# Moving half of the gated attention's values between two groups of output gates, and pacing its side work by columns

## The chip, the cores and the metric

The kernel runs on one core of a Trainium2 chip. Its engines are TensorE (PE, matrix products), VectorE (DVE), ScalarE (ACT), GpSimd (Pool) and SyncE (SP, which only starts transfers); each works through its own queue in order, and they meet at semaphores. The metric is the device time of one execution in microseconds.

## The reference

One layer of a decoder trunk on 512 tokens of 1024 channels, in float32. What matters here is its first part: one normalised input, one wide projection, and two token mixers that are gated and merged.

```python
h = rmsnorm(x, ln1)
hq, hk, hv, hr, ha, hatt, hgate = _split_cols(h @ w_in, SPLIT_SIZES)
log_a = log_sigmoid(ha @ w_a2 + b_a) / GLA_TAU
o = gla_mixer(q, k, v, log_a)            # 4 heads, chunks of 64 tokens
o = o * rsqrt(mean(o * o) + EPS) * gla_gn * silu(hr)
y_gla = o @ w_o_gla
...                                      # dilated attention gives y_att
mix = (sigmoid(g_gla) * y_gla + sigmoid(g_att) * y_att) @ w_out
x = x + mix
...                                      # MLP, gated embedding, last norm
```

## The kernel before

Every float32 product is made as three products of a rounded part (hi) and a rest (lo) of each operand, in the type fp32r. A weight block of 128 x 1024 is fetched by SP, its hi is made by ACT (L222), its lo by DVE (L217), two stages ahead of the products that read them (`weight`, `fetch`). The wide projections are done in a Strassen form (`strassen`): seven stages of 24 matmuls of 256 columns; sums of weight blocks are made by transfers that add (Pool, L194 and L205) and by DVE (L202, L208). At the end of stages 5, 6 and 7 a finished block is added up from PSUM by DVE (`add`, L326).

`run` (L233 to L237) issues matmuls in pieces of eight, and after each piece calls `step`. That does two things: it runs one function of the list `later` (short follow-up work of a projection: adds, sigmoids, splits), and it advances one generator of the list `side`, where two (`WAYS`) take turns. The side work is what PE has to do between the projections in small portions: softmax, and the gated linear attention, `gla(h)` for one head and `gla_out(h)` behind it. So the order of the instructions on every engine is fixed by how often `step` is called and by where the code appends to the two lists; nothing is scheduled at run time.

A head of `gla` has 16 steps. In the first four, ACT and DVE make exponentials of the decay and from them the scaled keys and queries (L820 to L844, the keys end with L840). Step 5 transposes the keys on PE (L852), step 6 makes the scores (L858, L860), step 7 splits the transposed keys (L864), steps 8 and 9 make the states (L812, then L881, L882, L886), steps 10 and 11 split these (L888 on ACT, L891 on DVE), steps 12 and 13 are the outputs (L812), and the rest their scale (L360, L361 on Pool, L918). It reads the values `gv0` (heads one and two) or `gv1` (three and four) split into hi and lo. `gla_out(h)` transposes two blocks of the result, multiplies them into the gates `rg` (L942) and has them split into `og`, the input of the products `og.0` to `og.7`.

The order of the projections here is oa (8 short ones), r0, r1, gv1, gb0, gb1, ga0, ga1, then og. Heads one and two run beside oa and r0, heads three and four beside gb0 and gb1. The gates r are put through a sigmoid on ACT and a product on DVE (`silu`, L994, L998), gb and ga through a sigmoid on ACT (L1003). `weights()` (L693 to L722) forms the weights of the three attention groups beside v0: small DVE operations up to cn (L711), then a transpose of it on PE (L714). All these tiles of 128 x 512 share one pool of 69 (`u32`, `NU`).

Of the kernel before, what the change touches and what calls it, by code (L numbers as in the profile page):

```python
# [22 lines left out]
KC = D // P  # L23
# [8 lines left out]
GQ, GK, GV, GR, GHA, ATT, GATE = 0, 512, 1024, 2048, 3072, 3088, 7696  # L32


def att_col(g, which):
    return ATT + (g * 3 + which) * 512
# [5 lines left out]
def weight_units():  # L42

    u = []

    def fm(name, src, col, n, row=0):
        for j in range(n):
            u.append((f"{name}.{j}", "fm", src, row, col + j * P))

    def tm(name, src, col):  # L50
        for i in range(4):
            u.append((f"{name}.{i}", "tm", src, i * 2 * P, col))

    fm("q0", "w_in", att_col(0, 0), 4)
    u = u[NS:]
    def quad(name, src, col, kind="quad"):
        for m, k in ((0, 0), (1, 0), (1, 1), (0, 1)):
            u.append((f"{name}.A{m + 1}{k + 1}", kind, src, k, col + m * (P if kind == "quad" else 256)))

    fm("k0", "w_in", att_col(0, 1), 4)  # L60
    fm("q1", "w_in", att_col(1, 0), 4)
    fm("k1", "w_in", att_col(1, 1), 4)
    quad("q2", "w_in", att_col(2, 0))
    quad("k2", "w_in", att_col(2, 1))
    tm("v1", "w_in", att_col(1, 2))
    tm("v2", "w_in", att_col(2, 2))
    quad("v0", "w_in", att_col(0, 2), "quadt")
    quad("gq", "w_in", GQ)
    quad("gk", "w_in", GK)
    quad("gv0", "w_in", GV, "quadt")  # L70
    for j in range(4):
        u.append((f"oa.{j}", "half", "w_o_attn", 0, j * 2 * P))
    quad("r0", "w_in", GR)
    quad("r1", "w_in", GR + 512)
    quad("gv1", "w_in", GV + 512, "quadt")
    for i in range(2):
        quad(f"gb{i}", "w_in", GATE + D + i * 512)
    for i in range(2):
        quad(f"ga{i}", "w_in", GATE + i * 512)
    fm("og", "w_o_gla", 0, 8)  # L80
    fm("wo", "w_out", 0, 8)
    for q in range(8):
        quad(f"m1q{q}", "w_mlp1", q * 512)
    for sub in range(2):
        for kk in range(16):
            u.append((f"m2s{sub}.{kk}", "tm", "w_mlp2", kk * 2 * P, sub * 512))
    for j in range(2):
        u.append((f"pp{j}.0", "tm", "w_pp", 0, j * 512))
    for j in range(2):
        tm(f"pg{j}", "w_pg", j * 512)  # L90
    return u
# [38 lines left out]
NU, NW, PIECE, WAYS = 69, 5, 8, 2  # L130
# [7 lines left out]
def block_kernel(ctx, tc, xT, ws, pT, wts, wha, wa2, vec, lnf, rel, onehot, ident_d, mask_d, out):  # L138
# [13 lines left out]
    def u32(name="u"):  # L152
        return ar.tile([P, T], F32, tag="u", name=name)
# [7 lines left out]
    def smt():  # L161
        return sm.tile([P, T], F32, tag="sm", name="smt")


    side, later = [], []

    def step():
        if later:
            later.pop(0)()
        if side:  # L170
            g = side.pop(0)
            if next(g, "end") != "end":
                side.insert(min(WAYS - 1, len(side)), g)

    def drain():
        while side or later:
            step()
# [55 lines left out]
    def run(mms, n=PIECE, shared=False):  # L233
        for i in range(0, len(mms), n):
            for o, l, r, a, b in mms[i:i + n]:
                TE.matmul(o, lhsT=l, rhs=r, start=a, stop=b, skip_group_check=shared)  # L236
            step()  # L237

    def three(ps, pairs):

# [35 lines left out]
    def halves(t):  # L276
        return slice(t * HT, (t + 1) * HT)
# [52 lines left out]
    def split_hi(x, col=None):  # L330
        hi = u32r()
        if col is None:
            S.activation(hi, x, AF.Copy)  # L333
        else:
            S.activation(hi, x, AF.Copy, scale=col)
        return hi

    def split_lo(x, hi, col=None):
        lo = u32r()
        if col is None:  # L340
            V.tensor_tensor(lo, x, hi.bitcast(F32), op=OP.subtract)  # L341
        else:
            V.scalar_tensor_tensor(out=lo, in0=x, scalar=col, in1=hi.bitcast(F32), op0=OP.mult, op1=OP.subtract)
        return hi, lo
# [5 lines left out]
    def split_later(x, res, j):  # L350

        def first():
            hi = split_hi(x)
            later.append(lambda: res.__setitem__(j, split_lo(x, hi)))
        later.append(first)
# [337 lines left out]
    def weights():  # L693

        def small(name):
            return st.tile([P, 16], F32, tag=name, name=name, bufs=1)

        nmx, e0, e1, e2, dn, cn1 = (small(n) for n in ("nmx", "e0", "e1", "e2", "dn", "cn1"))
        V.tensor_tensor(nmx, st0[:, 0, :], sn[:, 0, :], op=OP.min)
        V.tensor_tensor(e0, nmx, st0[:, 0, :], op=OP.subtract)  # L700
        V.tensor_tensor(e1, nmx, sn[:, 0, :], op=OP.subtract)
        S.activation(e0, e0, AF.Exp)
        S.activation(e1, e1, AF.Exp)
        yield
        yield
        V.tensor_tensor(e2, e0, st0[:, 1, :], op=OP.mult)
        V.tensor_tensor(dn, e1, sn[:, 1, :], op=OP.mult)
        V.tensor_tensor(dn, dn, e2, op=OP.add)
        V.reciprocal(dn, dn)
        V.tensor_tensor(cn0, e0, dn, op=OP.mult)  # L710
        V.tensor_tensor(cn1, e1, dn, op=OP.mult)  # L711
        yield
        pct = smt()
        TE.transpose(pct[0:16, 0:P], cn1, ident)  # L714
        yield
        ct = u32()
        V.tensor_copy(ct[0:16, 0:P], pct[0:16, 0:P])
        k_dram = dr.tile([4, T], F32, name="k_dram")
        GP.dma_start(k_dram.rearrange("h (b t) -> (h b) t", b=4), ct[0:16, 0:P])
        GP.dma_start(cc, k_dram.rearrange("h (m c) -> m h c", c=4))  # L720
        for _ in range(4):
            yield  # L722
# [211 lines left out]
    def gla_out(h):  # L934
        for f in range(2):
            j = 2 * h + f
            pts = smt()
            for p in range(4):
                TE.transpose(pts[:, p * P:(p + 1) * P],
                             ons_[h][p // 2][:, (p % 2) * 256 + f * P:(p % 2) * 256 + (f + 1) * P], ident)  # L940
            yield
            V.scalar_tensor_tensor(out=rg[j], in0=pts, scalar=cv[:, C_GN + j:C_GN + j + 1], in1=rg[j],  # L942
                                   op0=OP.mult, op1=OP.mult)
            split_later(rg[j], og, j)


    side.append(setup())
# [22 lines left out]
    gk = heads("gk", 1.0)  # L970
    gv = [values("gv0", True)]
    drain()
    side.extend(gla(h) for h in range(2))
    y_dram = dr.tile([KC, P, T], F32, name="y_dram")
    for j in range(KC):
# [3 lines left out]
    rg, tb, ga = [], [], []  # L979

    def gates(name, i, res, make):

        new = [u32() for _ in range(4)]
        res.extend(new)

        def finish(m, t, s, ps):
            add(m, s, s, ps)
            later.append(lambda: make([4 * i + 2 * n + m for n in range(2)], [new[2 * n + m][:, halves(t)] for n in range(2)], s, t))

        strassen(f"{name}{i}", xs_op, finish)  # L990
# [11 lines left out]
        for n in range(2):  # L1002
            S.activation(outs[n], s[:, halves(n)], AF.Sigmoid)  # L1003

    for i in range(2):
        gates("r", i, rg, silu)
    gv.append(values("gv1", True))
    while later:
        later.pop(0)()
    side.extend(gla(h) for h in range(2, 4))  # L1010
    side.extend(gla_out(h) for h in range(4))
    for i in range(2):
        gates("gb", i, tb, sigmoid)

# [5 lines left out]
            V.tensor_tensor(tb[j], tb[j], y, op=OP.mult)  # L1020
        return mult

    while later:
        later.pop(0)()
    later.extend(merge(j) for j in range(KC))
    for i in range(2):
        gates("ga", i, ga, sigmoid)
    drain()
    mix = [None] * KC
    for j in range(KC):  # L1030
        py = fm(f"og.{j}", og)
# [84 lines left out]
    while len(later) > 5:  # L1116
        step()
# [8 lines left out]
    def quad(q):  # L1126


        def finish(m, t, s, ps):
            add(m, s, s, ps)  # L1130

            def scale():
                o = s.rearrange("p (n t) -> p n t", n=2)
                V.scalar_tensor_tensor(out=o, in0=o, scalar=0.0,  # L1134
                                       in1=norm2[1][:, None, halves(t)].to_broadcast([P, 2, HT]),
                                       op0=OP.max, op1=OP.mult)

            def act():
                for n in range(2):
                    j = 4 * q + 2 * n + m  # L1140
                    if hid[j] is None:
                        hid[j] = u32()
                    S.activation(hid[j][:, halves(t)], s[:, halves(n)], AF.Square)  # L1143

            later.extend([scale, act])

        def extra(i):
            if i in (3, 4):
                later.append(lambda: hid_split(i - 3))

        strassen(f"m1q{q}", x1_op, finish, extra=extra if q == 7 else None)
# [3 lines left out]
    def hid_split(k):  # L1155
        if k < 32:
            hs[k] = split(hid[k])
# [10 lines left out]
    for sub in range(2):  # L1168
# [22 lines left out]
        for o in range(4):  # L1191
            j = 4 * sub + o
# [172 lines left out]
```

## Time and profile before

| | before |
|---|---|
| median of 3 runs | 1001.27 us (1000.89 to 1001.27) |
| profiled execution | 1003.71 us |
| its span | 1001.9 us |
| PE busy | 982.5 us |
| DVE busy | 673.1 us |
| ACT busy | 524.9 us |
| Pool busy | 80.3 us |
| mean granted PE clock | 0.993 of full speed |

The span runs from the first to the last instruction of the profiled execution; what lies around it is the rest of that execution's time. Busy times of different engines lie beside each other, so they don't add up to the span. What counts for an engine is how long it stood before an instruction, and for what.

### The profile page before, as it was taken

What the parts mean: (1) busy time and instruction counts of PE and PEld (TensorE: products, weight loads), DVE (VectorE), ACT (ScalarE), POOL (GpSimd) and SP (SyncE); (2) the same over time, 40 slices, a digit from 0 to 9 for tenths busy, and PEclk for the clock granted to TensorE, in tenths of its full rate; (3) what the DMA queues carried; (4) which work ended last, traced back from release to release, by engine and by line L of the source; (5) the groups of instructions that cost most, each with busy time, mean ns of one, the idle gap of its engine ahead of it and who ended that gap; (6) DMA issues with size and microseconds to landing.
All of it is one profiled execution on the core that took longest, in us unless ns stands there. A gap on an engine that the chain in (4) does not pass through costs nothing.

```text
span 1001.9 us, 15523 instructions
## 1 busy us (share of the span) xinstructions
PE 982.5 (98%) x6228; PEld 897.4 (90%) x6228; DVE 673.1 (67%) x948; ACT 524.9 (52%) x875; POOL 80.3 (8%) x116
## 2 busy tenths in 40 slices
PE   9999999999999999899999999999999999999996
PEld 7788999999998999899988889999998888888885
DVE  7777675566767677869855688778868444743554
ACT  7335547745455675766632346555656344442633
POOL 0230000010001101022002001001000000000000
PEclk9999999999999999899999999999999999999999
DMA  8463461464365355426636425655554322533102
GB/s 304 130 211 86 106 168 43 107 140 114 85 169 148 125 137 141 124 66 188 190 91 203 127 58 138 170 163 143 153 156 139 105 85 84 151 101 106 43 1 84
DMA packets 38168, 127.31 MB, mean 127 GB/s; under 512 B 4883, under 2 KB 6495, under 8 KB 38096
## 3 DMA queue, kind: packets, MB, share of 16 engines
q1 hardware_dynamic: 27504, 92.51, 28.1%
q0 software_dynamic: 8864, 30.66, 15.7%
q10 hardware_dynamic: 1728, 3.15, 0.8%
q8 instruction: 49, 0.80, 0.3%
q14 instruction: 23, 0.19, 0.1%
HBM read 122.06 MB, written 6.07 MB: 128 GB/s over the span
## 4 chain that ended last, share of the span: by engine, by line
PE 91%; DVE 5%; issue 2%; ACT 1%; DMA 0%; POOL 0%; SPq 0%; POOLq 0%; DVEq 0%; ACTq 0%
PE mmt L236 73%; PE smt L236 9%; DVE lo L217 1%; PE smt L812 1%; PE smt L756 1%; PE smt L683 1%; PE smt L858 1%; PE mmt L450 1%; DVE w L202 0%; PE mmt L451 0%; PE mmt L449 0%; DMA u<-in_xT_dram 0%; PE smt L860 0%; DVE ur L341 0%; PE smt L773 0%
## 5 line engine op out<-in xcount | busy, mean ns | idle before, releaser
L236 PE MATMUL mmt<-ur,hi 128*128 128x256 f32 (+1 forms) x2784 | 610.5, 315 | 0.0
L236 PEld LDWEIGHTS mmt<-ur,hi 128*128 128x128 f32 x2784 | 461.4, 192 | 31.9 <-issue 1.9
L236 PE MATMUL mmt<-ur,lo 128*128 128x256 f32 (+1 forms) x1392 | 438.2, 315 | 0.5 <-DVE lo L217 0.5
L217 DVE TENSOR_TENSOR lo<-w,hi 128x1024 fp32r<-128x1024 f32 x230 | 278.9, 1220 | 123.9 <-PE mmt L236 72.3
L222 ACT ACTIVATE hi<-w 128x1024 fp32r<-128x1024 f32 x230 | 240.4, 1053 | 132.0 <-issue 65.3
L236 PEld LDWEIGHTS mmt<-ur,lo 128*128 128x128 f32 x1392 | 266.8, 192 | 16.3 <-DVE lo L217 0.9
L236 PE MATMUL mmt<-hi,ur 128*128 128x256 f32 (+1 forms) x640 | 156.1, 334 | 0.0
L333 ACT ACTIVATE ur<-u 128x512 fp32r<-128x512 f32 x136 | 80.2, 621 | 89.3 <-DVE u L1033 30.9
L236 PEld LDWEIGHTS mmt<-hi,ur 128*128 128x128 f32 x640 | 119.8, 215 | 5.6
L236 PE MATMUL mmt<-lo,ur 128*128 128x256 f32 (+1 forms) x320 | 106.2, 332 | 0.6 <-DVE lo L217 0.6
L341 DVE TENSOR_TENSOR ur<-u,ur 128x512 fp32r<-128x512 f32 x135 | 89.0, 686 | 25.1 <-ACT ur L333 21.9
L236 PE MATMUL smt<-ur,hi 128*128 128x512 f32 x272 | 83.7, 389 | 0.0
L308 ACT ACTIVATE u<-mmt 128x512 f32<-128x512 f32 x84 | 49.9, 594 | 56.5 <-PE mmt L236 56.2
L326 DVE TENSOR_TENSOR u<-u,mmt 128x512 f32<-128x512 f32 (+1 forms) x84 | 52.5, 651 | 29.4 <-PE mmt L236 29.3
L236 PEld LDWEIGHTS mmt<-lo,ur 128*128 128x128 f32 x320 | 68.8, 215 | 3.6 <-DVE lo L217 1.0
L236 PEld LDWEIGHTS smt<-ur,hi 128*128 128x128 f32 x272 | 51.1, 188 | 10.6
L236 PE MATMUL smt<-ur,lo 128*128 128x512 f32 x136 | 53.0, 390 | 0.0
L205 POOL DMA_DIRECT2D w<-in_wts_dram x21 | 18.2, 868 | 314.5 <-DVE w L202 230.7
L1143 ACT ACTIVATE u<-u 128x256 f32<-128x256 f32 x64 | 23.0, 409 | 37.1 <-DVE u L1134 37.1
L194 POOL DMA_DIRECT2D w<-in_wts_dram x21 | 18.6, 888 | 204.7 <-DMA w<-in_wts_dram 94.5
L236 PEld LDWEIGHTS smt<-ur,lo 128*128 128x128 f32 x136 | 25.5, 188 | 5.3
L202 DVE TENSOR_TENSOR w<-w 128x1024 f32<-128x1024 f32 x21 | 25.7, 1225 | 0.7
(204 smaller groups left out, 718.3 us busy)
## 6 DMA issues: line engine op xcount, KB each, us to landing
w<-in_wts_dram SPq DMA_DIRECT2D x167, 512.0 KB, 3.7
w<-in_wts_dram POOLq DMA_DIRECT2D x42, 512.0 KB, 5.7
u<-in_xT_dram SPq DMA_DIRECT2D x8, 256.0 KB, 4.8
y_dram<-u ACTq DMA_DIRECT2D x8, 256.0 KB, 3.0
u<-y_dram POOLq DMA_DIRECT2D x8, 256.0 KB, 5.8
u<-in_xT_dram POOLq DMA_DIRECT2D x8, 256.0 KB, 7.6
cb_dram<-c_dram POOLq DMA_DIRECT2D x4, 448.0 KB, 5.9
u<-in_ws_dram SPq DMA_DIRECT2D x8, 192.5 KB, 4.7
```

Of the source, the lines that this page charges most:

```text
L194: GP.dma_start(w, wts[UNIT[f"{q}.A22"]], accum_op=OP.add)
L202: V.tensor_tensor(w, w, raw[f"{q}.A11"], op=OP.add)
L205: GP.dma_start(w, wts[UNIT[f"{q}.A21"]], accum_op=OP.add)
L217: V.tensor_tensor(lo, w, hi.bitcast(F32), op=OP.subtract)
L222: S.activation(hi, w, AF.Copy)
L236: TE.matmul(o, lhsT=l, rhs=r, start=a, stop=b, skip_group_check=shared)
L308: S.activation(sums[c], bank[b], AF.Copy, scale=-scale if c[0] else scale)
L326: V.tensor_tensor(out, s, ps, op=OP.subtract if m else OP.add)
L333: S.activation(hi, x, AF.Copy)
L341: V.tensor_tensor(lo, x, hi.bitcast(F32), op=OP.subtract)
L450: TE.matmul(q0ps[i], lhsT=hi[:, c], rhs=xl, start=False, stop=False)
L1143: S.activation(hid[j][:, halves(t)], s[:, halves(n)], AF.Square)
```

## The change

Five edits in the same file. First, `step` takes a number of columns: `later` is served at each call as before, the side work only once `pace` columns of matmuls have gone by. A piece of eight 512-column matmuls has 4096 columns, one of eight 256-column matmuls 2048. The pace is 2048 at first, 4096 from the end of gv0 to the end of ga1, then 2048 again; `drain` calls without columns and steps every time. Second, gv1 moves from behind r1 to between r0 and r1, in the code and in the list of weights. Third, `gla_out` of heads one and two starts with gv1, `gla` of heads three and four with r1, and their `gla_out` is queued behind. Fourth, `gla_out` no longer has its result split; a generator of its own, `gla_split`, does that for all eight blocks, queued between ga0 and ga1. Fifth, `weights()` has one more empty step ahead of its transpose.

```diff
     quad("r0", "w_in", GR)
+    quad("gv1", "w_in", GV + 512, "quadt")
     quad("r1", "w_in", GR + 512)
-    quad("gv1", "w_in", GV + 512, "quadt")
...
-    def step():
+    pace, since = [2048], [0]
+
+    def step(columns=None):
         if later:
             later.pop(0)()
-        if side:
+        since[0] += columns or pace[0]
+        if side and since[0] >= pace[0]:
+            since[0] = 0
             g = side.pop(0)
...
-            step()
+            step(PIECE * r.shape[-1])
...
         V.tensor_tensor(cn1, e1, dn, op=OP.mult)
         yield
+        yield
         pct = smt()
...
+    def gla_split():
+        for j in range(KC):
             split_later(rg[j], og, j)
+            yield
...
     drain()
+    pace[0] = 4096
     side.extend(gla(h) for h in range(2))
...
-    for i in range(2):
-        gates("r", i, rg, silu)
+    gates("r", 0, rg, silu)
+    flush()
+    side.extend(gla_out(h) for h in range(2))
     gv.append(values("gv1", True))
-    while later:
-        later.pop(0)()
+    flush()
     side.extend(gla(h) for h in range(2, 4))
-    side.extend(gla_out(h) for h in range(4))
+    gates("r", 1, rg, silu)
+    flush()
+    side.extend(gla_out(h) for h in range(2, 4))
...
     for i in range(2):
         gates("ga", i, ga, sigmoid)
+        if i == 0:
+            side.append(gla_split())
     drain()
+    pace[0] = 2048
```

(`flush` runs `later` until it is empty.) The file gets 18 lines longer; the lines named in this document are those of the kernel before, and in the rows of the changed order they are 4 to 10 higher (L217 is L221 there, L341 is L345, L820 is L825, L942 is L947).

On DVE, at the start of heads three and four, the order before is this, from the last split of gv1 on (names as built; u_1642 and u_1679 are the decays of the two heads):

```order
L341 TENSOR_TENSOR ur_4210<-u_4078,ur_4206 128x512
L217 TENSOR_TENSOR lo_4216<-w_4103,hi_4167 128x1024
L820 TENSOR_TENSOR u_4230<-u_1642 128x4x64
L822 TENSOR_TENSOR u_4231<-u_1642 128x4x64
L820 TENSOR_TENSOR u_4244<-u_1679 128x4x64
L822 TENSOR_TENSOR u_4245<-u_1679 128x4x64
L827 COPY dec_4257<-u_4229 128x8
L828 TENSOR_TENSOR u_2149<-u_2149,u_4229 128x512
L217 TENSOR_TENSOR lo_4265<-w_3860,hi_4218 128x1024
L208 TENSOR_TENSOR w_3860<-w_3860,w_4171 128x1024
L827 COPY dec_4281<-u_4243 128x8
L828 TENSOR_TENSOR u_2150<-u_2150,u_4243 128x512
```

and this in the changed kernel, again from the last split of gv1 on:

```order
L345 TENSOR_TENSOR ur_3989<-u_3832,ur_3985 128x512
L221 TENSOR_TENSOR lo_3995<-w_3859,hi_3939 128x1024
L947 SCALAR_TENSOR_TENSOR u_3361<-smt_3955,cv_118,u_3361 128x512
L221 TENSOR_TENSOR lo_4025<-w_3530,hi_3997 128x1024
L212 TENSOR_TENSOR w_3530<-w_3530,w_3943 128x1024
L825 TENSOR_TENSOR u_4042<-u_1642 128x4x64
L827 TENSOR_TENSOR u_4043<-u_1642 128x4x64
L825 TENSOR_TENSOR u_4064<-u_1679 128x4x64
L827 TENSOR_TENSOR u_4065<-u_1679 128x4x64
L221 TENSOR_TENSOR lo_4069<-w_3943,hi_4027 128x1024
L832 COPY dec_4094<-u_4041 128x8
L833 TENSOR_TENSOR u_2149<-u_2149,u_4041 128x512
```

Before, the third head's keys (L837 to L840) follow at once. In the changed order one more lo (L221) and the two rows of the fourth head (L832, L833) come first. One L947 and two more lo now stand between the splits of gv1 and the third head's keys; the stage beside which this runs is r1, not gb0.

The second place is on DVE too, later in the same two heads, where the states are finished (L886) and split (L891). Before:

```order
L882 SCALAR_TENSOR_TENSOR u_4541<-u_4540,dab_4282,smt_4498 128x256
L217 TENSOR_TENSOR lo_4551<-w_4100,hi_4487 128x1024
L202 TENSOR_TENSOR w_4100<-w_4100,w_4323 128x1024
L326 TENSOR_TENSOR u_4446<-u_4446,mmt_4270 128x512
L886 SCALAR_TENSOR_TENSOR u_4519<-u_4520,dab_4258,smt_4526 128x256
L886 SCALAR_TENSOR_TENSOR u_4540<-u_4541,dab_4282,smt_4547 128x256
L891 TENSOR_TENSOR ur_4521<-u_4519,ur_4521 128x256
L891 TENSOR_TENSOR ur_4522<-u_4520,ur_4522 128x256
L891 TENSOR_TENSOR ur_4523<-u_4519,ur_4523 128x256
L217 TENSOR_TENSOR lo_4601<-w_4435,hi_4553 128x1024
```

and in the changed kernel, where L887, L891 and L896 are the same three lines:

```order
L887 SCALAR_TENSOR_TENSOR u_4557<-u_4556,dab_4125,smt_4493 128x256
L221 TENSOR_TENSOR lo_4575<-w_4159,hi_4533 128x1024
L206 TENSOR_TENSOR w_4159<-w_4159,w_4393 128x1024
L330 TENSOR_TENSOR u_4491<-u_4491,mmt_4348 128x512
L891 SCALAR_TENSOR_TENSOR u_4520<-u_4521,dab_4095,smt_4527 128x256
L891 SCALAR_TENSOR_TENSOR u_4556<-u_4557,dab_4125,smt_4563 128x256
L221 TENSOR_TENSOR lo_4622<-w_4480,hi_4577 128x1024
L330 TENSOR_TENSOR u_4404<-u_4404,mmt_4300 128x512
L330 TENSOR_TENSOR u_4446<-u_4446,mmt_4300 128x512
L896 TENSOR_TENSOR ur_4522<-u_4520,ur_4522 128x256
L896 TENSOR_TENSOR ur_4523<-u_4521,ur_4523 128x256
L896 TENSOR_TENSOR ur_4524<-u_4520,ur_4524 128x256
```

The finished states and their splits stood next to each other; now a lo and the last two adds of the projection stand between them. On PE, the first outputs of head three come 40 matmuls of the projection after the last state product of head four before, and 80 now.

## Rows read from the trace of the kernel before

**Rows 1.** The page, busy time, share of the span, instructions.
```profile
PE 982.5 (98%) x6228; PEld 897.4 (90%) x6228; DVE 673.1 (67%) x948; ACT 524.9 (52%) x875; POOL 80.3 (8%) x116
```
**Rows 2.** Waits of PE: us in total, times, longest.
```profile
PE smt L852 <- DVE u L840: 2.9, 1, 2.9
PE smt L392 <- ACT ur L333: 1.6, 1, 1.6
PE smt L812 <- DVE ur L891: 1.3, 2, 1.0
...
PE smt L714 <- DVE cn L711: 1.0, 1, 1.0
...
PE smt L812 <- ACT ur L888: 0.4, 1, 0.4
```
**Rows 3.** Windows: length, busy time (instructions) by engine, granted PE clock, DMA, GB/s.
```profile
359.40:379.55 20.15, 20.15 (x170) 20.15 (x170) 17.31 (x23) 11.77 (x17) 2.39 (x3) 1.00 0.57 157
379.55:399.70 20.15, 20.15 (x170) 20.15 (x170) 15.76 (x20) 11.39 (x16) 1.76 (x3) 1.00 0.59 157
399.70:446.00 46.30, 41.73 (x312) 39.74 (x311) 38.49 (x69) 29.86 (x64) 4.66 (x7) 0.93 0.39 92
446.00:504.90 58.90, 58.90 (x495) 58.73 (x494) 47.11 (x57) 38.21 (x70) 9.52 (x14) 1.00 0.61 179
411.00:417.00 6.00, 5.75 (x27) 5.52 (x27) 5.90 (x14) 3.93 (x8) 0.35 (x1) 0.50 0.75 162
608.00:612.00 4.00, 3.78 (x17) 3.38 (x17) 3.88 (x4) 4.00 (x6) 0.00 (x0) 0.57 0.99 189
```
**Rows 4.** The chain that ended last, 405 to 430: start, length, what.
```profile
411.25 0.90 PE smt L852 x3
412.15 1.71 PE mmt L236 x8
413.86 0.64 PE smt L852 x3
...
416.20 0.32 PE smt L858 x2
...
418.96 1.15 PE mmt L236 x8
420.11 0.17 PE smt L858 x2
...
422.41 3.07 PE mmt L236 x24
...
426.20 0.96 PE mmt L236 x8
```
**Rows 5.** DVE in order of time, 400 to 412: start, length, instruction.
```profile
400.36 1.28 DVE L326 TENSOR_TENSOR u<-u,mmt 128x512 f32<-128x512 f32 x2
...
409.17 0.68 DVE L837 TENSOR_TENSOR u<-u 128x512 f32<-128x512 f32 x1
...
410.90 0.29 DVE L840 COPY u<-u 128x256 f32<-128x256 f32 x1
```
**Rows 6.** Groups of instructions by form: busy time, mean ns, idle before.
```profile
L217 DVE TENSOR_TENSOR lo<-w,hi 128x1024 fp32r<-128x1024 f32 x230 | 278.9, 1220 | 123.9 <-PE mmt L236 72.3 <-PE smt L236 31.2 <-ACT hi L222 18.9
L341 DVE TENSOR_TENSOR ur<-u,ur 128x512 fp32r<-128x512 f32 x135 | 89.0, 686 | 25.1 <-ACT ur L333 21.9 <-issue 2.7
...
L326 DVE TENSOR_TENSOR u<-u,mmt 128x512 f32<-128x512 f32 x68 | 45.0, 682 | 24.7 <-PE mmt L236 24.6
...
L998 DVE TENSOR_TENSOR u<-u 128x256 f32<-128x256 f32 x16 | 6.1, 420 | 5.0 <-ACT u L994 5.0
```
**Rows 7.** Waits of ACT and DVE, 300 to 600: total, times, longest.
```profile
ACT ur L888 <- PE smt L812: 5.5, 1, 5.5
...
DVE u L998 <- ACT u L994: 5.0, 4, 2.9
```
**Rows 8.** ACT in order of time, 424 to 426.
```profile
424.94 0.61 ACT L333 ACTIVATE ur<-u 128x512 fp32r<-128x512 f32 x1
425.57 1.28 ACT L1003 ACT_TABLE_LOAD   x1
```
**Rows 9.** PE in order of time, at the transpose of cn, with its wait.
```profile
207.35 0.27 PE L714 MATMUL smt<-ident,cn 128*16 128x128 f32 x1 [1.03 <-DVE cn L711]
```

More of the change, by code (lines that the diff above doesn't have):

```diff
@@ L1003, in sigmoid, with flush @@
             S.activation(outs[n], s[:, halves(n)], AF.Sigmoid)
-    for i in range(2):
-        gates("r", i, rg, silu)
+    def flush():
+        while later:
+            later.pop(0)()
+    gates("r", 0, rg, silu)
+    flush()
+    side.extend(gla_out(h) for h in range(2))
     gv.append(values("gv1", True))
-    while later:
-        later.pop(0)()
+    flush()
     side.extend(gla(h) for h in range(2, 4))
-    side.extend(gla_out(h) for h in range(4))
+    gates("r", 1, rg, silu)
+    flush()
+    side.extend(gla_out(h) for h in range(2, 4))
     for i in range(2):
@@ L1021, in merge @@
         return mult
-    while later:
-        later.pop(0)()
+    flush()
     later.extend(merge(j) for j in range(KC))
```

## The prediction

> **What bounds the kernel now.** I read the page's busy line first: TensorE (PE) is busy for 982.5 of 1001.9 us [rows 1]. A change that moves instructions and adds none can therefore gain only what PE loses between them, and by running below its full clock. The view of PE's waits says where it loses: the longest wait, 2.9 us, is for L840, the last of the four vector instructions that form the scaled keys of a gated-attention head [rows 2]. The windows by stage say when. In the chain eight matmuls, one piece, take 0.96 us [rows 4], so a stage of 21 pieces takes 20.15 us. Counted back from the wait (it ends at 411.25, lasted 2.9 us, and nine pieces stand before it), gb0 begins at 399.70. The two windows of 20.15 us before that, r1 and gv1, have PE busy throughout, and so has the one from 446.00 to the end of ga1. The one between, in which heads three and four of the gated attention run beside gb0 and gb1, has PE busy for 41.73 of 46.30 us and a mean granted clock of 0.93 [rows 3]. So the change is judged on this stretch, and on one wait of 1.0 us at L714 [rows 2].
>
> The chain of waits shows the stretch from inside. VectorE (DVE) works without a pause from the adds at 400.36 to the end of the first L840 at 411.19 [rows 5]; PE stands at the transposes L852 and starts them at 411.25. [...]
>
> **The change part by part.** Nothing is added or removed: 950 vector, 832 scalar, 121 Pool and 6059 PE instructions stand in both orders, with 12 table loads in each.
>
> *The third and fourth head at half pace, beside r1 and gb0 in place of gb0 and gb1.* With a pace of 4096 columns, a piece of eight 256-column matmuls (2048) steps the side work every second time. Before, the first transposes of head three come after nine pieces of their stage, 8.6 us; now they come after 20 pieces of r1, 20 x 0.96 = 19.2 us. What DVE does before them hardly grows. Before, it ends 411.19 - 399.70 = 11.5 us after the stage began. The order of DVE now has one L942 and two splits of weights (lo, L217) more between the adds and L840. Taken at 0.68 us (the form of L326) and 1.22 us [rows 6], that is 11.5 + 0.68 + 2 x 1.22 = 14.6 us. 14.6 against 19.2: the wait goes, with 4.6 us to spare. Worth: 2.9 us of waiting [rows 2], and the slow clock behind it. That is summed from the chain [rows 4]: two stretches of eight matmuls lose 1.71 - 0.96 = 0.75 us each (one row stands for both); the two groups of transposes lose half of 0.90 and 0.64 us, 0.8 together; the third head's score matmuls took from 416.20 to 418.96 = 2.76 us, those of the fourth at full clock 420.11 to 422.41 = 2.30, so 0.5. Together 2.8 us. Its bounds: 0, if the clock falls at another place instead, and 2.9, half of the 5.75 us that PE was busy at 0.50 from 411 to 417 [rows 3]. I take 2.8.
>
> *The same heads, second half.* Three waits at L812 for the splits of the states (L888 on ScalarE, ACT, and L891 on DVE) cost 0.4 + 1.3 = 1.7 us [rows 2]. ACT waited 5.5 us at L888 for PE's own L812 [rows 7]: by the built order all 69 tiles of the pool were in use, and the tile for a state came free only by the matmuls just ahead of the ones that read that state. Now two pieces lie between the steps, and the one tile that still comes free only by such a matmul is read 48 matmuls (5.8 us) later. The 1.7 us go too; bounds 0 (the pool stays the cause) and 1.7.
>
> *One more yield in weights().* PE stood 1.03 us at L714 for cn [rows 9]. One more piece of 0.96 us ahead of L714 fills it; about 0.95 us go. Behind L714 on PE are matmuls whose weights are ready; DVE's copy of the transposed weights, and the split of weights behind it, wait as long as before. Bounds: 0 and 1.03.
>
> *gv1 ahead of r1; the gated outputs split in ga1.* gv1 and r1 are the same 168 matmuls either way, and their loads on SyncE's queue only swap places. On Pool's queue three of the four rsqrt (L361) of heads three and four now stand behind the first weight sum of ga1 (L194) and the fourth behind the second of ga0 (L205); that one waits for a vector sum which stands ahead of rv on DVE in any case, so nothing late is put ahead of them. The eight splits of og (eight L341 at 0.69 us, 5.5 us [rows 6]) move into ga1. In the window that ends with ga1 DVE has 58.90 - 47.11 = 11.8 us free [rows 3], and that covers them. If that cover were gone, og.0 would wait: it needs the last split only at its 22nd matmul. Cost nil; bounds 0 and 1 us.
>
> *The price: DVE in r1 and early gb0.* r1 now has the sigmoid-times-value products (L998, eight), the splits of gv1 at its head, and a third of two heads' work. The tightest point by the order is the lo of gb0's third product. After the 14.6 us come four more lo (4.9 us), one weight sum of the same size (1.2), the fourth head's keys (2.0, as the third's from 409.17 to 411.19 [rows 5]), four L326 (2.7), the scaled queries of both heads (six small rows, taken at 1.2) and eight L998 (8 x 0.42 = 3.4) [rows 6]: 30.0 us. The waits for sigmoids come on top, which were 5.0 us in four places before [rows 7]; off come up to 2 us, since in the chain the rows follow each other some 0.08 us closer than they last. That makes 28 to 35 us, and I take 30.5, since DVE comes to most of these products late and finds the sigmoid done. PE asks for this lo after 20.2 us of r1, two groups of transposes (0.8), six pieces (5.8) and two sets of score matmuls (4.6): 31.4 us. It fits, barely: cost 0, at worst 3.6 us of waiting.
>
> ACT's table switch lies in that run: exponentials early in r1, then sigmoids, as before at gb0. The row shows 1.28 us for the load, started within 0.02 us of the end of the split ahead of it [rows 8]. [...]
>
> **Sum.** 2.9 + 2.8 + 1.7 + 0.95 = 8.35 us. The profiled execution took 1003.71 us (span 1001.9 and 1.8 around it), so after would be 995.4 in its own profile. The median of the timed runs, 1001.27, lies 2.4 below the profiled one; the same gain gives 992.9, and I say 993.0.
>
> **The rivals.**
>
> *A remnant stays.* The state splits still wait for a tile, or PE waits up to 2 us in gb0 for the lo above, and the clock does not fall. For it: by the built order the pool is still full in gb1, and the sum above is tight; against it: the spacing doubles. 994 to 997, say 995.
>
> *The stall only moves, with its clock.* The lag comes up in r1 or gb0 as a single wait of 3 us, and the clock falls as it did at 411: 2.9 + 2.8 are lost again, and 1.7 + 0.95 are kept: 998.6; without the 1.7, 1000.3: the change would not do what it says.
>
> *Slower.* DVE is overrun in r1 and gb0. It decides when waits for sigmoids and for ACT carry the 30.0 us past 34.4: then PE waits 3 us for the lo of gb0's third product, and as long for the keys' split (L864) of the third head that stands a few rows behind it, each time with 2.8 us of slow clock. 2 x 5.8 = 11.6 against the 8.35 saved: 1004.5. For it speak the 5.0 us [rows 7]; against it that DVE was ahead of ACT there, which it no longer is.
>
> *The fall of the clock near 608.* In a stage that the change does not touch PE waits 1.6 us at L392 [rows 2], and from 608 to 612 the granted clock is 0.57 [rows 3], which costs 4 x 0.43 = 1.7 us. The 1.0 us at L714 brought no fall. If this one fails to come, 991.3. [...] The trace has this wait once and cannot say.
>
> **How the numbers follow.** Forecast 993.0: 0.54 (its own range 992 to 994.2). Remnant 0.19. Near 608: 0.08. The stall moves: 0.12, of which half ends within 0.2% of before, about what a measurement of this kernel can tell from no change (999.3 to 1003.3). Slower: 0.07. So faster 0.87, same 0.06, slower 0.07. The range, 991.0 to 998.5, takes in the forecast, the remnant and the other clock, 0.81, and ends where the moved stall begins.
>
> **What would show it.** Right: no PE wait over 0.5 us between the end of oa and og.0, and a granted clock of 1.00 there; PE's wait at L714 under 0.2 us; the seven stages from r0 to ga1 together some 7.4 us shorter. Wrong: PE waiting in gb0 for lo or L864 (then the DVE sum was too low), ACT waiting for a tile at L888, or PE idle at the start of og.0 for a split. A wait of 2 us or more anywhere from r1 to gb1, with a clock of 0.50 behind it, makes the forecast wrong by 5 us.

## The result, and the profile after

The changed kernel takes 994.29 us (median of 4 runs, 993.96 to 995.67), the kernel before 1001.08 in the same comparison (4 runs, 1000.61 to 1001.27): a ratio of 0.9931 with a 95% interval of 0.992 to 0.9943, 6.8 us less. The forecast was 993.0 within 991.0 to 998.5. The profiled execution took 993.96 us.

In the changed file lines stand 4 to 18 further down: L217 is L221, L236 L240, L326 L330, L714 L719, L812 L817, L840 L845, L852 L857, L888 L893, L891 L896, L994 L1004, L998 L1008, L1003 L1013.

The page's busy line, which answers to [rows 1]:

```profile
PE 977.7 (99%) x6228; PEld 893.6 (90%) x6228; DVE 672.6 (68%) x948; ACT 524.6 (53%) x875; POOL 82.0 (8%) x116
```

With the span of 992.1 us PE stood idle for 992.1 - 977.7 = 14.4 us, against 1001.9 - 982.5 = 19.4 before. So half of the 9.8 us between these two executions is waiting (5.0) and half is shorter busy time of the same matmuls (4.8). Nearly all of the second half is the clock: the two low stretches of [rows 3] cost 2.9 and 1.7 us. And 0.8 us of the first half has nothing to do with the change: three short waits in the first 8 us (L449, L450), which the second profile of the kernel before, shown further down, doesn't have either. What PE waits for (engine, line, waited for: us in total, times, longest), against [rows 2]:

```profile
PE smt L396 <- ACT ur L337: 1.6, 1, 1.6
PE mmt L240 <- DVE lo L221: 1.2, 2, 0.6
PE smt L817 <- DVE ur L896: 1.1, 1, 1.1
PE smt L428 <- POOL ones L423: 1.0, 1, 1.0
PE smt L397 <- DVE ur L345: 0.2, 1, 0.2
```

The 2.9 us for the keys and the 1.0 us at the transpose of cn have no row any more. Of the 1.7 us before the heads' state matmuls and outputs 1.1 are left. The windows of the gated attention and of the second norm (columns as in [rows 3]):

```profile
350.00:400.00 50.00, 50.00 (x421) 50.00 (x420) 41.99 (x68) 34.92 (x67) 9.78 (x10) 1.00 0.51 127
400.00:450.00 50.00, 48.92 (x399) 47.64 (x398) 38.94 (x62) 30.06 (x65) 4.35 (x6) 1.00 0.50 127
596.00:600.00 4.00, 2.33 (x17) 1.82 (x15) 2.08 (x5) 1.29 (x3) 1.90 (x2) 1.00 0.47 138
600.00:604.00 4.00, 3.87 (x31) 3.83 (x32) 4.00 (x5) 3.65 (x6) 0.00 (x0) 1.00 0.95 221
```

The granted clock is 1.00 in all of them. The low clock behind the key stall (0.50 from 411 to 417 [rows 3]) is gone with the stall; the one behind the wait at L396 (L392 before, 0.57 from 608 to 612 [rows 3]) is gone too, though that wait is still 1.6 us long. The keys, on DVE, and their transposes, on PE, in order of time:

```profile
393.47 0.29 DVE L845 COPY u<-u 128x256 f32<-128x256 f32 x1
```
```profile
398.98 0.49 PE L857 MATMUL smt<-ident,u 128*128 128x128 f32 x3
```

The keys are ready at 393.76; PE comes to them at 398.98, 5.2 us later. Before, it came 2.9 us too early. The one wait that is left in this stretch, followed back from PE over DVE to ACT (the same columns, with the idle time before the row and what ended it):

```profile
436.64 1.00 PE L817 MATMUL smt<-ur 128*128 128x256 f32 x7
...
438.72 0.51 PE L817 MATMUL smt<-ur 128*128 128x256 f32 x2 [1.08 <-DVE ur L896]
```
```profile
435.84 1.23 DVE L221 TENSOR_TENSOR lo<-w,hi 128x1024 fp32r<-128x1024 f32 x1 [4.12 <-ACT hi L226]
437.10 1.23 DVE L212 TENSOR_TENSOR w<-w 128x1024 f32<-128x1024 f32 x1
438.25 1.09 DVE L896 TENSOR_TENSOR ur<-u,ur 128x256 fp32r<-128x256 f32 x3
```
```profile
434.44 0.42 ACT L893 ACTIVATE ur<-u 128x256 fp32r<-128x256 f32 x1 [4.71 <-PE smt L817]
434.77 1.04 ACT L226 ACTIVATE hi<-w 128x1024 fp32r<-128x1024 f32 x1
```

Read it from the last fence up. ACT stands for 4.71 us at the rounding of head four's third state, until PE has read head three's values (L817): by the built order the tile that ACT writes to is one of those. Behind ACT's row in its queue stands the hi of a weight; so DVE idles 4.12 us for that hi, then makes the lo and a weight sum, and only then the rests of the states, for which PE waits 1.08 us.

### The profile page after: what moved, and what is told of

The parts are those of the page before. It is cut to its first block, busy times and chain, and to the rows that moved or that the text cites. A ratio compares the mean times of both kernels' runs of the same rounds, so it can differ in the third digit from the quotient of the medians.

```text
span 992.1 us, 15516 instructions
## 1 busy us (share of the span) xinstructions
PE 977.7 (99%) x6228; PEld 893.6 (90%) x6228; DVE 672.6 (68%) x948; ACT 524.6 (53%) x875; POOL 82.0 (8%) x116
## 4 chain that ended last, share of the span: by engine, by line
PE 94%; issue 2%; DVE 2%; ACT 1%; DMA 0%; POOL 0%; POOLq 0%; DVEq 0%; SPq 0%; ACTq 0%
PE mmt L240 76%; PE smt L240 9%; PE smt L817 1%; DVE lo L221 1%; PE smt L761 1%; PE smt L687 1%; PE mmt L453 1%; PE mmt L454 1%; PE mmt L455 1%; PE smt L863 1%; PE smt L865 0%; PE smt L778 0%; PE smt L777 0%; PE smt L767 0%; PE smt L944 0%
## 5 line engine op out<-in xcount | busy, mean ns | idle before, releaser
L240 PE MATMUL mmt<-ur,hi 128*128 128x256 f32 (+1 forms) x2784 | 607.7, 314 | 0.0
L240 PEld LDWEIGHTS mmt<-ur,hi 128*128 128x128 f32 x2784 | 457.8, 190 | 31.9 <-issue 1.9
L240 PE MATMUL mmt<-ur,lo 128*128 128x256 f32 (+1 forms) x1392 | 436.7, 314 | 0.5 <-DVE lo L221 0.5
L221 DVE TENSOR_TENSOR lo<-w,hi 128x1024 fp32r<-128x1024 f32 x230 | 279.1, 1221 | 129.3 <-PE mmt L240 67.3
L240 PEld LDWEIGHTS mmt<-ur,lo 128*128 128x128 f32 x1392 | 264.0, 190 | 16.1 <-DVE lo L221 0.7
L240 PE MATMUL mmt<-hi,ur 128*128 128x256 f32 (+1 forms) x640 | 156.9, 334 | 0.0
L240 PEld LDWEIGHTS mmt<-hi,ur 128*128 128x128 f32 x640 | 120.1, 215 | 5.6
L240 PE MATMUL mmt<-lo,ur 128*128 128x256 f32 (+1 forms) x320 | 106.3, 332 | 0.6 <-DVE lo L221 0.6
L345 DVE TENSOR_TENSOR ur<-u,ur 128x512 fp32r<-128x512 f32 x135 | 89.1, 688 | 21.5 <-ACT ur L337 20.9
L240 PE MATMUL smt<-ur,hi 128*128 128x512 f32 x272 | 83.8, 389 | 0.0
L330 DVE TENSOR_TENSOR u<-u,mmt 128x512 f32<-128x512 f32 (+1 forms) x84 | 52.5, 652 | 32.7 <-PE mmt L240 32.7
L240 PEld LDWEIGHTS mmt<-lo,ur 128*128 128x128 f32 x320 | 68.9, 215 | 3.6 <-DVE lo L221 1.0
L240 PEld LDWEIGHTS smt<-ur,hi 128*128 128x128 f32 x272 | 51.1, 188 | 10.7
L240 PE MATMUL smt<-ur,lo 128*128 128x512 f32 x136 | 53.0, 390 | 0.0
L240 PEld LDWEIGHTS smt<-ur,lo 128*128 128x128 f32 x136 | 25.5, 188 | 5.2
```

The source lines that it names most:

```text
L221: V.tensor_tensor(lo, w, hi.bitcast(F32), op=OP.subtract)
L330: V.tensor_tensor(out, s, ps, op=OP.subtract if m else OP.add)
```

## The experiments

Every group of runs had the kernel before on the same chip beside it (1001.58, 1001.49 and 1001.40 us). Variants of different groups are compared by their ratios to it. The first group began with the changed kernel again.

> The changed kernel once more, as the yardstick of this call. Both theories: 0.993 of before (6.8 us less). What it is to tell: whether PE's one wait at the state splits (1.1 us) is there in every execution, and how much slow clock this one has near 600.

Measured: 994.96 us (994.52 to 996.04), ratio 0.9934 (0.9922 to 0.9947). The gain is repeated, and this is the reference for the variants of the changed kernel.

**The order without the pace.** From the changed kernel one line is taken away:

```diff
-    pace[0] = 4096
```

> The changed kernel without the new pace: gv1 stays between r0 and r1 and heads three and four run beside r1, but the side work steps after each piece. Theory (the spacing of a head's steps made the gain): the key transposes again come nine pieces into their stage, 8.6 us, before DVE's 11.5 us of work are done, so PE waits about 3 us with up to 2.8 us of slow clock behind it, and the waits at the state splits come back; 998 to 1000 where the changed kernel has 994.3. Rival (the place made it, beside r1 with DVE freer before it): within 1 us of the changed kernel.

Measured: 1002.66 us (1001.75 to 1004.70), ratio 1.0013 (1.0004 to 1.0022). The whole gain is gone, and more: I had expected 998 to 1000, and the extra step in `weights()`, worth about 1 us, is still in this kernel. Two waits of PE in order of time, and the windows at them:

```profile
392.26 0.55 PE L857 MATMUL smt<-ident,u 128*128 128x128 f32 x3 [3.16 <-DVE u L845]
...
420.72 0.58 PE L817 MATMUL smt<-ur 128*128 128x256 f32 x1 [2.46 <-DVE ur L896]
```
```profile
392.00:396.00 4.00, 3.69 (x20) 3.40 (x21) 3.90 (x11) 1.93 (x5) 0.00 (x0) 0.64 0.54 107
420.00:424.00 4.00, 3.28 (x16) 3.28 (x17) 3.96 (x8) 2.34 (x10) 0.04 (x1) 0.57 0.42 131
```

The key stall has moved with its heads from gb0 to r1 and has grown from 2.9 to 3.2 us; the splits of the states now cost 2.5 us in one piece, and a fall of the clock stands behind each (0.64 from 392 to 396, 0.57 from 420 to 424). So without the spacing the new place gives nothing. Whether the spacing would do as well in the old place is not shown: that wasn't tried.

**Only the keys given more time.** In the kernel before, two empty steps ahead of the transposes of heads three and four:

```diff
+        for _ in range(2 if h > 1 else 0):
+            yield
         kc = slice(0, 3 * P)
         pk = smt()
```

> The kernel before with nothing but two empty steps ahead of the key transposes of heads three and four (3.8 us more between the keys and their transposes). Theory: the wait of 2.9 us goes, and the slow clock behind it where an execution has it: 2.9 to 5.7 us less than before, 995.4 to 998.2; the waits at the state splits (1.7 us) stay or change by a microsecond. Rival (the gain came from the place of gv1): under 1 us.

Measured: 1004.41 us (1003.07 to 1007.15), ratio 1.003 (1.0021 to 1.0039): slower, where I expected 2.9 to 5.7 us less. PE's two long waits, and DVE before the first:

```profile
414.71 0.39 PE L236 MATMUL mmt<-ur,lo 128*128 128x256 f32 x1 [2.52 <-DVE lo L217]
...
442.53 0.51 PE L812 MATMUL smt<-ur 128*128 128x256 f32 x2 [3.22 <-DVE ur L893]
```
```profile
411.31 0.28 DVE L840 COPY u<-u 128x256 f32<-128x256 f32 x1
...
413.24 0.28 DVE L840 COPY u<-u 128x256 f32<-128x256 f32 x1
413.44 1.22 DVE L217 TENSOR_TENSOR lo<-w,hi 128x1024 fp32r<-128x1024 f32 x1
```

The transposes no longer wait for the keys. But the keys of both heads still stand in front of the lo of the next weights on DVE, and PE waits 2.5 us for that lo, until 414.71, where it stood for the keys until 411.25 before. The keys were only what PE met first: the backlog is all of DVE's work in the stretch, and moving one reader gives it no time. Further on the wait for the states' rests is 3.2 us in place of the 1.7 us of three waits. The granted clock of this profile is low behind both waits (0.62 from 416 to 420, 0.71 from 444 to 448); in the second profile of the kernel before it is low behind one (0.57 from 412 to 416). This speaks against the stall being a matter of order between two steps alone.

**The third state one step later.** In the changed kernel ACT's rounding of the third state moves behind the next yield:

```diff
-        for p in range(1, 4):
+        for p in range(1, 3):
             S.activation(ss[p][:, 0:256], s[p], AF.Copy)
         yield
+        S.activation(ss[3][:, 0:256], s[3], AF.Copy)
```

> The changed kernel with the hi of a head's third state made one step later, so that ACT no longer stands before a tile that only PE's outputs of the other head set free, with a hi and DVE's lo and weight sum queued behind it. Theory (the tile's wait on ACT, 4.7 us, is what delays the state splits): PE's wait of 1.1 us at the first outputs of head four goes, 1.0 us less than the changed kernel. Rival (DVE's own run is too long): PE waits as before, within 0.3 us of the changed kernel.

**One more tile.** In the changed kernel `NU` is 70, and `rstd` has one buffer in place of two to make room.

> The changed kernel with 70 tiles in the pool of 128x512 tiles in place of 69 (the space is taken from the second buffer of rstd). Theory: the last PE wait for head four's outputs (1.1 us at L817) comes from the third state's first split on ACT, which waits 4.7 us for a tile that only PE's outputs of head three give back. With one tile more ACT starts earlier and the wait goes: about 993.3 to 993.9, as the kernel with that split one step later (993.25). Rival: DVE's rows ahead of the splits are what is late; then the 1.1 us stay, and it takes 994.5 to 995.3. A second rival: rstd with one buffer makes Pool or ACT wait in the norms, 996 or more.

Measured: 993.25 us (993.20 to 994.81), ratio 0.9922 (0.9908 to 0.9935), with the third state later, and 993.65 us (992.62 to 994.59), ratio 0.9915 (0.9901 to 0.9929), with 70 tiles. Each interval overlaps that of the changed kernel, so the medians alone don't show a gain. The profiles do: neither has a row for L817 among PE's waits, and between two waits for a lo that all these kernels have, near 183 and 590 us (their rows are shown further down), both take 405.57 us in place of 406.97. With 70 tiles ACT starts the six roundings so:

```profile
424.80 0.71 ACT L893 ACTIVATE ur<-u 128x256 fp32r<-128x256 f32 x2
428.19 0.42 ACT L893 ACTIVATE ur<-u 128x256 fp32r<-128x256 f32 x1 [2.68 <-PE mmt L240]
...
429.12 1.01 ACT L893 ACTIVATE ur<-u 128x256 fp32r<-128x256 f32 x3
430.04 1.04 ACT L226 ACTIVATE hi<-w 128x1024 fp32r<-128x1024 f32 x1
```

The last has ended by 430.13, where it began at 434.44 in the changed kernel, and the hi stands right behind it. One more tile, or one step more for the row that waits for it, takes the 1.08 us away: it was the cause.

**The early splits put back.** In the changed kernel the outputs are split in `gla_out` again, as before; `gla_split` goes:

```diff
             V.scalar_tensor_tensor(out=rg[j], in0=pts, ...
-    def gla_split():
-        for j in range(KC):
             split_later(rg[j], og, j)
-            yield
...
-        if i == 0:
-            side.append(gla_split())
```

> The changed kernel with the splits of the gated outputs put back into the steps that form the outputs. The forecast costed this edit at nothing: within 0.5 us of the changed kernel (994.5 to 995.3), with the waits of PE as there. Rival: the eight splits (5.5 us of DVE) stand in front of rows for which PE waits in the last gates, and the wait at L817 of 1.1 us grows by one to three splits (0.7 to 2.1 us): 995.7 to 997.

Measured: 1000.10 us (999.14 to 1001.82), ratio 0.9985 (0.9976 to 0.9994). Five us are lost, more than twice what the rival allowed. PE at the outputs of the heads, then ACT and DVE in front of them:

```profile
435.94 0.96 PE L817 MATMUL smt<-ur 128*128 128x256 f32 x3 [0.39 <-ACT ur L893]
...
438.65 1.00 PE L817 MATMUL smt<-ur 128*128 128x256 f32 x7
...
442.53 0.50 PE L817 MATMUL smt<-ur 128*128 128x256 f32 x2 [2.88 <-DVE ur L896]
```
```profile
435.47 0.72 ACT L893 ACTIVATE ur<-u 128x256 fp32r<-128x256 f32 x2 [7.11 <-PE smt L817]
436.72 0.42 ACT L893 ACTIVATE ur<-u 128x256 fp32r<-128x256 f32 x1 [0.52 <-DVE ur L896]
```
```profile
435.92 0.76 DVE L896 TENSOR_TENSOR ur<-u,ur 128x256 fp32r<-128x256 f32 x2 [1.43 <-ACT ur L893]
437.17 0.43 DVE L896 TENSOR_TENSOR ur<-u,ur 128x256 fp32r<-128x256 f32 x1 [0.48 <-ACT ur L893]
439.65 1.23 DVE L221 TENSOR_TENSOR lo<-w,hi 128x1024 fp32r<-128x1024 f32 x1 [2.06 <-ACT hi L226]
```

DVE is not short of time here: it idles 1.4, 0.5 and 2.1 us for ACT. ACT waits 7.1 us for tiles. An output that is split holds two tiles (hi and rest), one that isn't holds one; where the outputs of heads one and two are formed while heads three and four are at work, their early splits take the tiles that the states need. By the built order all six roundings of the states then take a tile within nine of the projections' matmuls of its last use, as they do in the kernel before; in the changed kernel two do, and ACT waits at one. PE's waits are 2.6 us longer than in the changed kernel (L817 2.9 + 0.4 - 1.1, the lo 0.4). Between the two waits for a lo near 183 and 590 us this profile takes 410.85 us, 3.9 more than the changed kernel, with the clock at 1.00 all the way; the 1.3 us beyond the waits stay without a cause here. Behind that stretch the clock is at 0.65 from 604 to 608 and at 0.93 in the 4 us behind it, 1.4 + 0.3 = 1.7 us. That fall follows the wait at L396, which the edit doesn't touch, and it comes and goes in other kernels too; that the early splits bring it is not shown. So they cost about 4 us. A run with the early splits and more tiles, which would part the tiles from the order on DVE, wasn't made; for the tiles speak ACT's 7.1 us and DVE's idling.

**The late splits alone.** The same part, alone, in the kernel before: `gla_split` queued between ga0 and ga1.

> The kernel before with one part of the change alone: the gated outputs are split in the last gates' steps and not in those that form the outputs. Theory (tiles): in the changed kernel this part matters because the outputs of heads one and two are formed while heads three and four are still at work; their early splits hold tiles that the state splits need. In the kernel before all outputs are formed after head four, so the state splits find the pool as full as ever, and this part alone gives nothing: within 0.7 us of before (1000.8 to 1002.2), with the waits at L812 (0.4 and 1.3 us) as they were. Rival (DVE time): the 5.5 us of splits crowd DVE beside the gates wherever they stand; then moving them helps here too, and it takes 998 to 1000.

Measured: 1001.95 us (1000.75 to 1003.98), ratio 1.0007 (0.9999 to 1.0016). No gain, as the tiles want it: there, no output is formed before head four is done, and the waits at L812 are the old 1.3 and 0.4 us. This part of the change is worth something only beside another part.

**The extra step in weights() alone.** One `yield` more in the kernel before, ahead of the transpose of cn.

> The kernel before with the one more yield in weights() alone. Forecast's term: PE's wait of 1.0 us at L714 is filled by one more piece of 0.96 us, so the kernel takes 0.95 us less than before in the same runs (about 1000.6 where before is 1001.5), and the wait at L714 is under 0.2 us. Rival: the side work behind it all comes one piece later, and the wait comes back there or the clock falls at another place: within 0.5 us of before, or up to 1.7 us on either side if one more or one less fall of the clock comes with it.

Measured: 1000.23 us (999.22 to 1001.74), ratio 0.9985 (0.9976 to 0.9994), 1.3 us less than before (0.6 to 2.4 by the interval). The transpose, with no wait at its row:

```profile
207.15 0.27 PE L715 MATMUL smt<-ident,cn 128*16 128x128 f32 x1
```

**The kernel before, profiled again.**

> The kernel before, once more, for a second profile of it. Its first profiled execution took 1003.71 us with the granted clock low at two places, 411 to 417 us and 608 to 612 us (mean clock 0.993), while most of its timed runs take 1000.8 to 1002.2 at a mean clock of 0.995 or 0.996. One of the two falls is missing in those. Theory A: the one near 608 comes and goes, the one at 411 is always there. Then this profile has a span of about 1000.2 us, its clock is 0.50 for some 6 us behind the key stall, and the 2.8 us of the forecast's clock term are in the median too. Theory B: the one at 411 comes and goes. Then the span is about 999.1 to 999.5, the clock is 1.00 behind the key stall, the clock term belongs to the slowest runs alone, and the gain of the medians is what the waits alone give.

Measured: 1001.71 us (1000.35 to 1002.34), the profiled execution 1001.53 with a span of 999.7. The windows at the key stall and where the first profile had the second fall:

```profile
408.00:412.00 4.00, 1.09 (x10) 0.89 (x9) 3.79 (x9) 4.00 (x9) 1.89 (x3) 1.00 0.00 0
412.00:416.00 4.00, 3.85 (x21) 3.49 (x20) 4.00 (x11) 1.93 (x5) 0.00 (x0) 0.57 1.01 151
416.00:420.00 4.00, 4.00 (x29) 3.33 (x29) 2.68 (x4) 2.09 (x4) 0.00 (x0) 1.00 0.79 275
608.00:612.00 4.00, 4.00 (x35) 3.98 (x34) 3.90 (x5) 3.21 (x5) 0.00 (x0) 1.00 0.94 238
```

Theory A, with a smaller size than the first profile gave (the span of 999.7 lies between the two that were expected): the fall behind the key stall is there (4 x 0.43 = 1.7 us at most, against 2.8 to 2.9 in the first execution), the one near 608 is not. The first profile held more clock loss than the execution that gives the median.

**The gap in the second norm.** In the kernel with 70 tiles, outside what the change touches:

```diff
-    side.append(rms_gen(acc1, norm2, 6, 2))
+    side.append(rms_gen(acc1, norm2, 6, 3))
```

> The changed kernel with 70 tiles (as in the run of that name) and, in the second norm, a gap of three steps in place of two, so that the matmul of the norm (L396, for which PE waits 1.6 us and then 0.2 us) comes two pieces of 0.96 us later. Theory: the wait goes, 1.8 us, and with it the fall of the clock near 600, which some executions show and others don't (992.6 and 992.9 against 994.4 and 994.6 in the kernel with 70 tiles): all runs near 990.8 to 991.2, in one group. Rival 1: the norm comes later and the feed-forward's first matmuls wait for it as long: 992.6 to 994.6 as before this edit. Rival 2: the wait goes, but the fall comes elsewhere or has another cause: two groups again, near 990.9 and 992.7.

Measured: 991.94 us (991.58 to 992.65, 4 runs), ratio 0.9908 (0.9893 to 0.9923). PE's wait there:

```profile
599.02 0.50 PE L396 MATMUL smt<-ur,ones_r 128*128 128x512 f32 x1 [0.49 <-ACT ur L337]
599.75 0.50 PE L397 MATMUL smt<-ur,ones_r 128*128 128x512 f32 x1 [0.22 <-DVE ur L345]
```

Of 1.8 us 0.7 stay, so the time is 0.7 to 1.1 us above what I expected. The two groups of the kernel with 70 tiles (992.6 and 992.9, 994.4 and 994.6) have become one that is 1.1 us wide, which fits the theory that the longer wait sets off the fall in some executions; four runs don't prove it. This is the fastest of all the kernels, 9.5 us under the one before.

## Why the prediction was right, step by step

*What bounds the kernel, and the key stall (2.9 us).* Right. PE's idle time and its clock were all there was to gain, and most of what was gained lay in the stretch of heads three and four. The spare time of the keys was forecast as 4.6 us and is 5.2. The run without the pace shows that the new place doesn't do it without the spacing, and the run with the two empty steps that time for the keys alone doesn't either: it had to be spacing for all of DVE's work.

*The slow clock behind it (2.8 us).* Right in kind, too large for the median. It was read from an execution of 1003.71 us, and the forecast then took this gain from the median, 1001.27, as if every execution had it. In the second profile of before it is some 1.7 us. Counting a clock loss from one execution and subtracting it from the median of others was the weak step; the rival about the fall near 608 came from the same execution. That fall did fail to come, as in that rival, but it is missing from the second profile of before as well, an execution as long as the median, so I count it as no part of the gain.

*The state splits (1.7 us).* This step failed by two thirds: 0.6 us came. The prediction saw the one tile that still comes free late and said that its reader comes 5.8 us afterwards. It followed the tile to PE's read and left out ACT's queue between them: behind the row that waits for the tile stood a weight's hi, behind that DVE's lo and a weight sum, and behind these the rests of the states. From ACT's start at 434.44 to PE's start at 438.72 that chain takes 4.28 us; PE was there after 3.2. The rival "A remnant stays" gave its cause as the full pool, and its 994 to 997 holds the result, while 994.29 lies just above the 992 to 994.2 that the forecast gave itself. So by its time it is this rival that came, and by its cause for 1.1 us; the clock term, above, was too large by as much again. The stated range holds the result because it takes the rival in.

*The step in weights() (0.95 us).* Right: no wait at the transpose, and 1.3 us alone (0.6 to 2.4).

*The sum for the usual execution.* 2.9 + 1.7 + 0.6 + 0.95 = 6.2 us, against 6.8 measured at the medians (6.6 in the second comparison). The missing 0.4 to 0.6 is mostly a term that the sum lacked. In the row at 436.64 above seven matmuls take 1.00 us; one alone lasts 0.28, so the next begins 0.12 us after it. The stop behind that row therefore cost about 0.16 us more than its 1.08 us of idle time, which is counted from the end of the row. Three stops are gone in the stretch of heads three and four (the keys and two of the three at the states); if each cost as much, that is 0.5 us, an estimate.

*The late splits of the outputs: nil.* The result is right only because the change as a whole holds both parts. The prediction counted DVE's time for eight splits and looked for cover in ga1. What the part does, as far as the traces show it, is free tiles in gb0 and gb1; without it the changed kernel takes 5 us more, 4 of them in these stages, and with it alone the kernel before gains nothing. The prediction had the pool in front of it, in the step before, and didn't count the tiles here.

*The price in r1 and gb0: nil.* Right. No lo in gb0 was late. The one that the prediction called the tightest is the first of these two:

```profile
407.85 2.36 DVE L221 TENSOR_TENSOR lo<-w,hi 128x1024 fp32r<-128x1024 f32 x2
```

r1 began 19.2 us before the transposes at 398.98, at 379.78, so this lo ended 407.85 + 1.22 - 379.78 = 29.3 us after that; 30.5 were forecast. DVE's waits for sigmoids (us in total, times, longest) fell from 5.0 [rows 7], as the prediction took them to:

```profile
DVE u L1008 <- ACT u L1004: 2.4, 4, 0.8
```

The table switch is in the place that was foreseen. In the order of time on ACT:

```profile
393.71 1.06 ACT L226 ACTIVATE hi<-w 128x1024 fp32r<-128x1024 f32 x1
394.79 1.28 ACT L1004 ACT_TABLE_LOAD   x1
398.59 0.63 ACT L1004 ACTIVATE u<-u 128x512 f32<-128x512 f32 x1 [2.52 <-DVE u L330]
```

Again 1.28 us, begun 0.02 us after the row ahead of it, and the sigmoid behind it waits 2.52 us for DVE. Behind the load of [rows 8] the activation began at once:

```profile
426.86 0.42 ACT L1003 ACTIVATE u<-u 128x256 f32<-128x256 f32 x1
```

It starts 0.01 us after the load's end (425.57 + 1.28), and behind each of the 12 loads of that profile the activation starts within 0.02 us of the load's end. So no load there held up the row behind it by more than 1.30 us.

*What would show it.* "No PE wait over 0.5 us between the end of oa and og.0" was broken once, by the 1.08 us. The sign of being wrong "ACT waiting for a tile at L888" came as well, with the 4.71 us. The clock of 1.00 there and the empty row at the transpose of cn were as foreseen. For the stages from r0 to ga1 the two waits for a lo near 183 and 590 us serve as marks; the first lies ahead of every edit (PE, in order of time, of before and of after):

```profile
183.64 0.63 PE L236 MATMUL mmt<-lo,ur 128*128 128x512 f32 x1 [0.63 <-DVE lo L217]
...
598.62 0.39 PE L236 MATMUL mmt<-ur,lo 128*128 128x256 f32 x1 [0.52 <-DVE lo L217]
```
```profile
183.24 0.62 PE L240 MATMUL mmt<-lo,ur 128*128 128x512 f32 x1 [0.64 <-DVE lo L221]
...
590.21 0.39 PE L240 MATMUL mmt<-ur,lo 128*128 128x256 f32 x1 [0.53 <-DVE lo L221]
```

414.98 us became 406.97, 8.0 us less, 1.0 of it from weights(): 7.0 for the stages, where 7.4 was forecast against the same execution of before. The two are closer than their parts: the states gave 1.1 us less than forecast, and the stops cost more than their rows. From the second profile of before (414.15 us) it is 7.2 us less in all, and 6.2 for the stages. The run of the changed kernel that gives its second median (406.96 us here) passes the first mark 0.7 us later than that profile of before, where no edit reaches, and so ends 6.6 us ahead of it.

## What to carry to other kernels

When PE waits for a step of side work, ask first whether the engine that makes it is behind with everything: then a reader that is moved meets the next late row, and what helped here was more matmuls between all the steps. Count tiles as well as time for each edit, and follow a late tile through the queue of the engine that waits for it, not only to its reader. A gain in clock is read from two or three executions before it is taken from a median.

## What I had not expected of the hardware

Behind the same wait the clock falls in one execution and not in the next. The 1.6 us at L396 had the granted clock at 0.57 behind it in the first profile of before, at 1.00 in the second and in the changed kernel; of the eleven profiles that have this wait, three show the fall (the others are the late splits alone, 0.57 from 608 to 612, and the early splits put back, 0.65 from 604 to 608). With the early splits put back PE idled 2.9 us at L817, as long as at the key stall of before, and the clock there stayed at 1.00:

```profile
440.00:444.00 4.00, 1.47 (x12) 1.48 (x13) 3.97 (x6) 4.00 (x8) 0.00 (x0) 1.00 0.81 131
444.00:448.00 4.00, 4.00 (x35) 4.00 (x35) 2.63 (x4) 3.55 (x11) 0.71 (x1) 1.00 0.63 189
```

So one trace can't say whether a wait of this length costs the clock as well, and a median can hold executions of both kinds. What decides between the two, none of these rows shows.
